# An elementwise multiply and GELU on one core: DRAM rows of 128 KB in two stores, with narrowing steps, in place of three contiguous pieces

## The chip, the cores and the metric

One core of one Trainium2 chip. The time is the device time of one execution in microseconds (us); quoted are medians. The kernels that are compared ran on the same chip, in turn.

## The reference

```python
x, y: (1024, 4096) float32
z = x * y
return 0.5 * z * (1 + tanh(sqrt(2 / pi) * (z + 0.044715 * z ** 3)))
```

33.55 MB are read and 16.78 MB written. The work is elementwise, so any assignment of elements to partitions is right if x, y and the output have the same.

## The kernel before

Each of the 128 partitions holds 32,768 columns of x in `xs`, where the product and the result overwrite it. y doesn't fit beside it and comes in three loads into a buffer of 20,440 columns; the second and third overwrite parts of the first that the multiplies have used. Columns of one *piece* lie in DRAM as one contiguous block, so a partition's row in the piece (1280, 17664) is 64 KB long and the next partition's follows it directly.

```python
PIECES = [(0, 1280), (1280, 17664), (17664, 32768)]
Y_LOADS = [(1280, 17664, 4056), (17664, 32768, 0), (0, 1280, 15104)]   # columns a:b, place in ys
Y_FREE = [0, 3, 4]                              # multiplies that must be done before the load
STEPS = [[4096] * 4, [2048] * 7 + [768], [1280]]
STORES = [(1280, 17664), (17664, 32768), (0, 1280)]

def columns(t, a, b):                           # piece [pa, pb) is contiguous in DRAM
    flat = t.flatten_outer_dims().rearrange("r c -> (r c)")
    pa, pb = next(q for q in PIECES if q[0] <= a and b <= q[1])
    return flat[P * pa : P * pb].rearrange("(p c) -> p c", p=P)[:, a - pa : b - pa]

_hoist(nc, [load_x(0).ins])                     # SyncE's queue, the very first
_hoist(nc, [load_x(1, nc.scalar).ins])          # ScalarE's queue
load_y(0)                                       # all others on SyncE's queue
load_x(2)
for i in range(1, len(Y_LOADS)):
    if Y_FREE[i]:
        nc.sync.wait_ge(sem_mul, Y_FREE[i])
    load_y(i)
# ... per step: VectorE xs = xs * ys, then ScalarE xs = gelu(xs) ...
for i, (a, b) in enumerate(STORES):
    if i == 0:
        nc.sync.wait_ge(sem_y[-2], 16)          # the first store waits for the second y load
    nc.sync.wait_ge(sem_act, done[b])
    nc.sync.dma_start(out=columns(out, a, b), in_=xs[:, a:b]).then_inc(sem_o[i], 16)
```

## Time and profile before

| | before |
|---|---|
| time, median (first 3 runs) | 119.83 us (119.72 to 119.94) |
| profiled execution, span | 118.3 us |
| VectorE, ScalarE busy | 35.2, 31.0 us |
| DMA queues, share of 16 engines | 82.2% + 16.5% |
| transfers, of which with 5 KB rows | 9, 3 |

A *packet* is one row of one partition, moved by one of the 16 DMA engines; a *wave* is 16 packets of one size, one per engine; a transfer has *landed* when its semaphore says that all of it is there.

Read the table from the bottom: the 16 DMA engines are full, so only two things can move the time, how many microseconds of rows each engine has to move, and any moment in which it moves none. The profile's lines stand in the prediction.

### The profile page before, as it was taken

What the parts mean: (1) busy time and instruction counts of PE and PEld (TensorE: products, weight loads), DVE (VectorE), ACT (ScalarE), POOL (GpSimd) and SP (SyncE); (2) the same over time, 40 slices, a digit from 0 to 9 for tenths busy, and PEclk for the clock granted to TensorE, in tenths of its full rate; (3) what the DMA queues carried; (4) which work ended last, traced back from release to release, by engine and by line L of the source; (5) the groups of instructions that cost most, each with busy time, mean ns of one, the idle gap of its engine ahead of it and who ended that gap; (6) DMA issues with size and microseconds to landing.
All of it is one profiled execution on the core that took longest, in us unless ns stands there. A gap on an engine that the chain in (4) does not pass through costs nothing.

```text
span 118.3 us, 82 instructions
## 1 busy us (share of the span) xinstructions
DVE 35.2 (30%) x13; ACT 31.0 (26%) x14; POOL 0.2 (0%) x4
## 2 busy tenths in 40 slices
DVE  0000000000000069999920000059999940000000
ACT  4000000000000001977974000007998990000000
POOL 0000000000000000000000000000000000000000
DMA  9888899889988897797797797798899889977975
GB/s 493 382 382 382 355 643 421 355 355 532 532 355 355 355 654 327 327 654 327 327 654 327 327 654 327 327 576 355 355 643 421 355 355 429 552 327 327 654 327 222
DMA packets 1296, 50.33 MB, mean 426 GB/s; under 512 B 144, under 2 KB 144, under 8 KB 528
## 3 DMA queue, kind: packets, MB, share of 16 engines
q1 hardware_dynamic: 1152, 41.94, 82.2%
q10 hardware_dynamic: 144, 8.39, 16.5%
HBM read 33.55 MB, written 16.78 MB: 426 GB/s over the span
## 4 chain that ended last, share of the span: by engine, by line
DMA 53%; DVE 24%; ACT 3%; issue 1%; DVEq 0%
DMA ys<-in_y_dram 53%; DVE xs L97 24%; ACT xs L105 3%; DVEq L94 0%
## 5 line engine op out<-in xcount | busy, mean ns | idle before, releaser
L97 DVE TENSOR_TENSOR xs<-xs,ys 128x2048 f32<-128x2048 f32 (+3 forms) x13 | 35.2, 2778 | 60.7 <-DMA ys<-in_y_dram 60.7
L105 ACT ACTIVATE xs<-xs 128x2048 f32<-128x2048 f32 (+3 forms) x13 | 29.7, 2301 | 64.9 <-DVE xs L97 64.9
L105 ACT ACT_TABLE_LOAD x1 | 1.3, 1283 | 1.6 <-PEq L59 1.6
L135 POOL MEMSET const-bfloat16-1.0<- 128x1 bf16 x1 | 0.1, 102 | 0.0
L135 POOL MEMSET const-uint8-127<- 128x1 uint8 x1 | 0.1, 102 | 0.0
L135 POOL MEMSET const-float32-0.0<- 128x1 f32 x1 | 0.1, 99 | 0.2 <-issue 0.2
L135 POOL MEMSET const-float32-1.0<- 128x1 f32 x1 | 0.1, 99 | 0.0
## 6 DMA issues: line engine op xcount, KB each, us to landing
xs<-in_x_dram SPq DMA_DIRECT2D x1, 7552.0 KB, 58.2
ys<-in_y_dram SPq DMA_DIRECT2D x1, 7552.0 KB, 22.5
out_dram<-xs SPq DMA_DIRECT2D x1, 7552.0 KB, 20.4
xs<-in_x_dram SPq DMA_DIRECT2D x1, 640.0 KB, 13.3
ys<-in_y_dram SPq DMA_DIRECT2D x1, 640.0 KB, 19.7
out_dram<-xs SPq DMA_DIRECT2D x1, 640.0 KB, 20.8
xs<-in_x_dram ACTq DMA_DIRECT2D x1, 32.5
ys<-in_y_dram SPq DMA_DIRECT2D x1, 40.7
```

The costliest lines, as they stand in the source:

```text
L97: nc.vector.tensor_mul(out=xs[:, c : c + w], in0=xs[:, c : c + w], in1=ys[:, r + c - a : r + c - a + w],).then_inc(sem_mul, 1)
L105: nc.scalar.activation(out=xs[:, c : c + w], in_=xs[:, c : c + w], func=GELU).then_inc(sem_act, 1)
L135: nc = _bacc.Bacc("TRN2", target_bir_lowering=False, num_devices=1)
```

## The change

Its intent: x, y and the output are seen as 128 rows of 128 KB, without the pieces. The output then leaves in two stores with equal rows of 64 KB, and no store of 5 KB rows is left at the end. Since all of the second half must be computed before its one store, the last steps are made narrow, so that ScalarE, which follows VectorE, has little left when VectorE ends. The small 5 KB loads remain: the heads of x first, the tails of y last.

```diff
-PIECES = [(0, 1280), (1280, 17664), (17664, 32768)]
-Y_LOADS = [(1280, 17664, 4056), (17664, 32768, 0), (0, 1280, 15104)]
+X_LOADS = [(0, 1280), (1280, 16384), (16384, 32768)]
+Y_LOADS = [(0, 16384, 4056), (16384, 31488, 0), (31488, 32768, 15104)]
-STEPS = [[4096] * 4, [2048] * 7 + [768], [1280]]
-STORES = [(1280, 17664), (17664, 32768), (0, 1280)]
+STEPS = [                                       # (y load, first column, width)
+    *((0, c, 4096) for c in range(0, 16384, 4096)),
+    (1, 16384, 1536), (1, 17920, 2048), (2, 31488, 1280),
+    *((1, c, 2048) for c in range(19968, 28160, 2048)),
+    (1, 28160, 1280), (1, 29440, 1024), (1, 30464, 640), (1, 31104, 384),
+]
+STORES = [(0, 16384), (16384, 32768)]
 def columns(t, a, b):
-    flat = t.flatten_outer_dims().rearrange("r c -> (r c)")
-    pa, pb = next(q for q in PIECES if q[0] <= a and b <= q[1])
-    return flat[P * pa : P * pb].rearrange("(p c) -> p c", p=P)[:, a - pa : b - pa]
+    return t.flatten_outer_dims().rearrange("(p a) c -> p (a c)", p=P)[:, a:b]
 # (cut: the loops over steps and stores, rewritten for the new tables, same waits)
```

More of the change, by code (lines that the diff above doesn't have):

```diff
@@ L10 @@
 GELU = mybir.ActivationFunctionType.Gelu_apprx_tanh
-PIECES = [(0, 1280), (1280, 17664), (17664, 32768)]
-Y_LOADS = [(1280, 17664, 4056), (17664, 32768, 0), (0, 1280, 15104)]
+COLUMNS = 32768
+X_LOADS = [(0, 1280), (1280, 16384), (16384, 32768)]
+Y_LOADS = [(0, 16384, 4056), (16384, 31488, 0), (31488, 32768, 15104)]
 Y_FREE = [0, 3, 4]
-STEPS = [[4096] * 4, [2048] * 7 + [768], [1280]]
-STORES = [(1280, 17664), (17664, 32768), (0, 1280)]
+STEPS = [
+    *((0, c, 4096) for c in range(0, 16384, 4096)),
+    (1, 16384, 1536),
+    (1, 17920, 2048),
+    (2, 31488, 1280),
+    *((1, c, 2048) for c in range(19968, 28160, 2048)),
+    (1, 28160, 1280),
+    (1, 29440, 1024),
+    (1, 30464, 640),
+    (1, 31104, 384),
+]
+STORES = [(0, 16384), (16384, 32768)]
 Y_BUF = 20440
@@ L51, in columns @@
     def columns(t, a, b):
-        flat = t.flatten_outer_dims().rearrange("r c -> (r c)")
-        pa, pb = next(q for q in PIECES if q[0] <= a and b <= q[1])
-        return flat[P * pa : P * pb].rearrange("(p c) -> p c", p=P)[:, a - pa : b - pa]
+        return t.flatten_outer_dims().rearrange("(p a) c -> p (a c)", p=P)[:, a:b]
     tc.close()
     tc.compile()
-    xs = nc.alloc_sbuf_tensor("xs", [P, PIECES[-1][1]], F32).ap()
+    xs = nc.alloc_sbuf_tensor("xs", [P, COLUMNS], F32).ap()
     ys = nc.alloc_sbuf_tensor("ys", [P, Y_BUF], F32).ap()
-    sem_x = [nc.alloc_semaphore(f"sem_x{i}") for i in range(len(PIECES))]
+    sem_x = [nc.alloc_semaphore(f"sem_x{i}") for i in range(len(X_LOADS))]
     sem_y = [nc.alloc_semaphore(f"sem_y{i}") for i in range(len(Y_LOADS))]
@@ L69, in load_x @@
     def load_x(i, engine=nc.sync):
-        a, b = PIECES[i]
+        a, b = X_LOADS[i]
         return engine.dma_start(out=xs[:, a:b], in_=columns(x, a, b)).then_inc(sem_x[i], 16)
@@ L86 @@
         load_y(i)
-    n = 0
-    done = {}
-    for i, (a, b, r) in enumerate(Y_LOADS):
-        for j, (xa, xb) in enumerate(PIECES):
-            if xa <= a < xb:
-                nc.vector.wait_ge(sem_x[j], 16)
-        nc.vector.wait_ge(sem_y[i], 16)
-        c = a
-        for w in STEPS[i]:
-            nc.vector.tensor_mul(
-                out=xs[:, c : c + w],
-                in0=xs[:, c : c + w],
-                in1=ys[:, r + c - a : r + c - a + w],
-            ).then_inc(sem_mul, 1)
-            n += 1
-            done[c + w] = n
-            nc.scalar.wait_ge(sem_mul, n)
-            nc.scalar.activation(
-                out=xs[:, c : c + w], in_=xs[:, c : c + w], func=GELU
-            ).then_inc(sem_act, 1)
-            c += w
+    waited = set()
+    for n, (i, c, w) in enumerate(STEPS, 1):
+        needed = [sem_y[i]] + [
+            sem_x[j] for j, (xa, xb) in enumerate(X_LOADS) if xa < c + w and c < xb
+        ]
+        for sem in needed:
+            if sem.num not in waited:
+                waited.add(sem.num)
+                nc.vector.wait_ge(sem, 16)
+        a, b, r = Y_LOADS[i]
+        nc.vector.tensor_mul(
+            out=xs[:, c : c + w],
+            in0=xs[:, c : c + w],
+            in1=ys[:, r + c - a : r + c - a + w],
+        ).then_inc(sem_mul, 1)
+        nc.scalar.wait_ge(sem_mul, n)
+        nc.scalar.activation(
+            out=xs[:, c : c + w], in_=xs[:, c : c + w], func=GELU
+        ).then_inc(sem_act, 1)
     for i, (a, b) in enumerate(STORES):
@@ L112 @@
             nc.sync.wait_ge(sem_y[-2], 16)
-        nc.sync.wait_ge(sem_act, done[b])
+        nc.sync.wait_ge(sem_act, max(n for n, (_, c, _) in enumerate(STEPS, 1) if a <= c < b))
         nc.sync.dma_start(out=columns(out, a, b), in_=xs[:, a:b]).then_inc(sem_o[i], 16)
```

## The prediction

> **What bounds the kernel now.** I read the first page for balance, then the DMA part for how many transfers there are, then stretches of the span for the rate, and last the chain of waits and the order in time around the first and last stores.
>
> ```profile
> span 118.3 us, 82 instructions
> DVE 35.2 (30%) x13; ACT 31.0 (26%) x14; POOL 0.2 (0%) x4
> DMA packets 1296, 50.33 MB, mean 426 GB/s; under 512 B 144, under 2 KB 144, under 8 KB 528
> ...
> q1 hardware_dynamic: 1152, 41.94, 82.2%
> q10 hardware_dynamic: 144, 8.39, 16.5%
> ```
>
> No compute engine is busy for a third of the span; the two DMA queues together take 98.7% of what 16 engines could give. 1296 packets are nine transfers of 128 rows and 16 semaphore writes. Three of them (the first x load, the last y load, the last store) have 5 KB rows: 3 x 128 = 384 of the 528 packets under 8 KB; the other 144 are the semaphore writes.
>
> The rate by stretch (the columns: stretch, its length, busy time of the three compute engines, the TensorE clock, the DMA share of 16 engines, GB/s; a packet is booked whole where it ends, which is why I chose stretches that hold exactly one wave of 16 packets):
>
> ```profile
> 1.00:118.00 117.00, 35.21 (x13) 31.01 (x14) 0.00 (x0) 1.00 1.00 430
> 80.50:82.50 2.00, 2.00 (x1) 1.83 (x1) 0.00 (x0) 1.00 1.21 524
> 99.50:102.00 2.50, 0.00 (x0) 0.00 (x0) 0.00 (x0) 1.00 0.89 387
> 116.40:117.60 1.20, 0.00 (x0) 0.00 (x0) 0.00 (x0) 1.00 1.02 418
> ```
>
> From 1 to 118 us the DMA engines are busy all the time. The second line is a wave of the first store: 524 x 2.00 = 1048 KB, which is 16 rows of 65,536 B, over 1.21 x 2.00 = 2.42 us on each engine. The third is a wave of the second store: 387 x 2.50 = 968 KB, 16 rows of 60,416 B, over 2.23 us. Both are 27.1 GB/s per engine, 433 GB/s for sixteen. The packet records of the trace say the same singly: 2,418 ns for 64 KB, 2,229 ns for 60,416 B, and 196 ns for most 5 KB rows. The first two differ by 5,120 B and 189 ns, so 5 KB cost 189 ns by size alone; as a row of its own it pays 7 ns more. Loads and stores have the same durations, and so have rows at a 64 KB pitch (x1, y0, the first store) and at 60,416 B. So at this rate DRAM isn't what limits; the 16 engines are.
>
> Then the end of the kernel, first the chain of waits (start, length, what), then the order in time:
>
> ```profile
> 55.54 22.47 DMA ys<-in_y_dram
> ...
> 78.10 1.52 DVE xs L97
> 79.62 0.68 issue
> 80.31 13.31 DVE xs L97 x6
> ...
> 93.64 3.80 ACT xs L105 x3
> ```
>
> ```profile
> 96.30 0.34 SPq L114 DMA_DIRECT2D out_dram<-xs  x1
> ...
> 97.46 0.33 SPq L114 DMA_DIRECT2D out_dram<-xs  x1
> ```
>
> The chain blames VectorE for 24% of the span, and that misleads. The second half of the compute (78.10 to 97.44) lies beside the first store, which is issued at 78.02. The packet records show that store's last rows ending between 98.27 and 98.51, and the second store's first rows starting on the same engines at 98.27 to 98.51, with no gap. The second store had been issued at 96.30, 2 us early; the third (5 KB rows) at 97.46, 18.7 us before its first packet at 116.13. The last packet ends at 117.88 and its semaphore comes at 118.25. Per engine the sum of rows is 3 x 8 x (2,418 + 2,229 + 196) = 116.23 us; from the first packet at 1.01 to the last at 117.88 are 116.87. The 0.64 left are mostly the offset between the engines' starts. There is practically no idle time to win.
>
> **What the Trainium skill says.** *DMA: Bandwidth & Descriptors*, "Where 436 GB/s comes from", puts the ceiling at 435 GB/s (16 ports); the trace's 433 agrees. The same page, "Latency and other measured facts", under "HBM row pitch at large powers of two", has copies with a per-partition pitch of 512 KiB at 207 GB/s per direction, 2 MiB at 164, full being 214. The changed kernel's pitch is 128 KB, a fourth of the mildest of these; the trace of before has no such pitch, only 64 KB, where nothing is lost. *ScalarE: Activation LUTs*, "What ACT_TABLE_LOAD costs", gives 186 ns + 0.833 ns per column for one ACTIVATE and an overlap of about 93 ns back to back. The trace agrees: 827 ns for 768 columns (826), 1,253 for 1280 (1,252), and the last three take 3.80 us where their durations sum to 3.99. *VectorE: DVE Perf Modes*, "Specifications", gives 0.96 GHz, 2,133 ns for 2048 columns at one a cycle; in the trace the starts are 2,202 ns apart, so one instruction costs columns/0.96 + 69 ns.
>
> **The change, part by part.**
>
> 1. *Bytes.* The same 50.33 MB. x is 5,120 + 60,416 + 65,536 B per row in place of 5,120 + 65,536 + 60,416; y has the same three sizes; the output is two stores of 64 KB rows for three. A row of 60,416 and one of 5,120 become part of one row of 65,536: 2,229 + 196 - 2,418 = 7 ns, eight rows per engine: **0.06 us less** on the path that sets the end. This is the only certain gain.
>
> 2. *Start of compute.* The first step needs x0, x1 and y0. Ahead of the compute there are now 8 x (196 + 2,229 + 2,418) = 38.7 us per engine and no longer 8 x (196 + 2 x 2,418) = 40.3, so the first multiply should start near 40.9 and not at 42.41. It saves nothing: the first store must stay behind the y loads in the queue, and until the end of the second y load the sum of rows is unchanged, so that one still lands near 78.0. The second and third y loads will be issued about 1.5 us earlier (near 54.0 and 58.4), both before the x load ahead of them ends at 59.8, so the queue doesn't run dry, as it doesn't now.
>
> 3. *First store.* Its issue after the landing at 78.0 is hidden by eight 5 KB rows (1.57 us per engine): issue at 78.02, first packets at 78.86 to 79.19. Unchanged.
>
> 4. *Second half of the compute.* Eleven steps for nine, 2 x 69 = 0.14 us more of VectorE. Starts from 78.10: the 1280 columns that follow the four of 2048 start at 92.18, then 93.58 (1024), 94.72 (640), 95.46 (384), end 96.01. ScalarE, with the formula above: 2048 until 94.21, then 1280 until 95.37, 1024 until 96.31, 640 until 96.93, 384 until **97.34**. So ScalarE, not VectorE, closes the half, and all of the second store waits for it: issue at 97.36. Now the corresponding store goes out at 96.30, so 1.06 us of the lead are lost. This is the one place where the change can cost time. From issue to first packet took 78.86 - 78.02 = 0.84 us, so the earliest packet can be at 98.20; the first engine becomes free at 98.27. It fits by 0.07 us. The narrowing widths are what makes it fit. I put the idle time at **0 to 0.2 us**.
>
> 5. *End.* Eight waves of 2,418 ns from 98.27 to 98.51 end at 117.61 to 117.85, in place of 117.88 at the latest; the semaphore about 0.37 us later, as now. One semaphore wait less on SyncE at the end, off the path.
>
> Sum: -0.06 + 0.0 to 0.2, on a median of 119.83: 119.8 to 120.0 by this account. Some of these waits may be half as large as I read them, so I take 119.8.
>
> **The rivals.**
>
> - *The 128 KB pitch slows DRAM.* For it: in both halves all rows now lie at one power of two, and the skill's page shows losses at pitches of powers of two. Against it: a 64 KB pitch loses nothing (2,418 ns, exactly what the size predicts), the engines run 0.2 to 0.5 us apart, which spreads their addresses, and the ceiling of the engines leaves DRAM some slack before a loss shows. 3% on every transfer would be 3.5 us, about 123.3; 3% on the stores alone 1.2 us, about 121.0. I give it one chance in fifteen of showing at all.
> - *The late second store leaves a hole.* If ScalarE ends later than I work out or the start of a transfer takes 1.2 us and not 0.84, all engines idle for some 0.4 us: 120.2. For it: the margin is 0.07 us. Against it: it needs an error in two durations that fit to some nanoseconds.
> - *Earlier compute or fewer small rows bring a real gain.* 1.5 us earlier compute would make 118.3, if it reached the end. Against it: the queue is full from 1.01 us on; VectorE gaining 1.5 us in the first half only waits longer for y1. A gain above 2% (under 117.4) needs a rate above 433 GB/s, which no stretch of whole waves shows.
>
> **Range and chances.** The before runs spread over 0.22 us; another chip or session may add as much. 119.4 to 120.4 takes in the gain of 0.06 with a fast session and the hole of 0.4 with a slow one; the pitch rival is outside it. Faster by over 2%: 1%. Slower by over 2% (over 122.2): only if all transfers lose by pitch, 3%.
>
> **What would show it.** Right: DMA packets 1152 (eight transfers), under 8 KB 384; a first multiply near 40.9; the second-half multiply still near 78.1; the second store issued near 97.4; waves of 64 KB still 2.42 us; DMA share near 1.0 up to 118. Wrong: 64 KB rows longer than 2.45 us (pitch), a share clearly below 1 around 98 us (hole), a y1 landing that isn't near 78.0 (then my reading of the queue is wrong).

## The result

| | before | after |
|---|---|---|
| median of 6 runs | 119.81 us (119.72 to 119.94) | 120.14 us (119.99 to 120.19) |
| profiled execution: time, span | 119.62, 118.3 us | 120.18, 118.8 us |
| second y load has landed | 78.00 | 78.63 |
| last store has landed | 118.25 | 118.81 |
| from the one to the other | 40.25 | 40.19 |

The ratio is 1.0026 (95% interval 1.0013 to 1.0039): the same within 2%, but slower by about 0.3 us. Ratios here are the mean time of one kernel's fast runs over that of the other's in the same rounds, so not quite the ratio of the medians quoted. The two profiled executions differ by 0.56 us, more than the medians; times inside a profile are compared with that in mind.

The page of the changed kernel, in the lines that answer those of before:

```profile
span 118.8 us, 83 instructions
DVE 35.3 (30%) x15; ACT 31.1 (26%) x16; POOL 0.2 (0%) x4
DMA packets 1152, 50.33 MB, mean 424 GB/s; under 512 B 128, under 2 KB 128, under 8 KB 384
...
q1 hardware_dynamic: 1008, 42.60, 83.4%
q10 hardware_dynamic: 144, 7.73, 15.0%
```

Eight transfers of 144 packets, the same bytes, the same compute. The stretches of the changed kernel (columns as in the prediction): the whole, one wave of the first store, one of the second.

```profile
1.00:118.00 117.00, 35.35 (x15) 31.09 (x16) 0.00 (x0) 1.00 1.00 430
81.00:83.00 2.00, 2.00 (x2) 1.28 (x2) 0.00 (x0) 1.00 1.21 524
...
100.00:102.40 2.40, 0.00 (x0) 0.00 (x0) 0.00 (x0) 1.00 1.01 437
```

A correction to the prediction first: it says that a packet is booked whole where it ends. It is booked where it *starts*; the wave in the second line starts at 81.94 by its packet records, that in the third at 101.31. A stretch that holds one whole wave reads the same either way, so the rates stand. Both waves are 16 rows of 64 KB in 2.42 us (1.21 x 2.00 and 1.01 x 2.40), as before. Rows at a 128 KB pitch are moved as fast as contiguous ones. So the rate in the body did not change.

The chain of waits of the changed kernel, and the issue of the second store from its order in time:

```profile
54.56 24.06 DMA ys<-in_y_dram
...
78.65 14.18 DVE xs L106 x7
...
92.86 5.05 ACT xs L112 x5
```

```profile
97.94 0.34 SPq L120 DMA_DIRECT2D out_dram<-xs  x1
```

54.56 + 24.06 = 78.62: the second y load lands 0.6 us later than before, and everything behind it moves with it: VectorE's half from 78.10 to 78.65, the second store's issue to 97.94. After that landing the changed kernel needs 0.06 us *less*. The time was lost before 78 us, in a stretch with the same bytes and the same waits (the sizes of the x and y loads only come in another order).

Most of it was lost in the first two microseconds. The kernel before, then the changed kernel, from 1 to 3 us:

```profile
1.00:2.00 1.00, 0.00 (x0) 0.43 (x1) 0.00 (x0) 1.00 0.95 374
2.00:3.00 1.00, 0.00 (x0) 0.85 (x1) 0.00 (x0) 1.00 2.68 1084
```

```profile
1.00:2.00 1.00, 0.00 (x0) 0.43 (x1) 0.00 (x0) 1.00 0.94 184
2.00:3.00 1.00, 0.00 (x0) 0.85 (x1) 0.00 (x0) 1.00 2.41 1006
```

In the first line of each only 5 KB rows of x start. The engines are as busy (0.95 and 0.94 of the time, the last column but one), yet the rows begun are 374 KB before and 184 KB after: 73 rows and 36. The same rows take longer. 190 KB less over 16 engines at 27.1 GB/s are 0.44 us per engine. (The 1084 and 1006 aren't rates: long rows of x that start there are booked whole; only stretches with short rows can be read as a rate.) The packet records show it singly. A 5 KB row takes 196 ns once the engines run; among the first ones of the changed kernel some took up to 1,001 ns, before at most 291. The last engine to begin its first long row of x did so at 3.31 us and not at 2.49. The packet records name no engine, so that one can't be followed. But the first long rows end 0.8 us apart over the 16 engines (before: 0.5), the last rows of the second y load still 0.7 us apart, the last of them at 78.18 and not at 77.64 (on average 0.4 us later than before), and the first store waits for that load as a whole.

### The profile page after: what moved, and what is told of

It reads as the page before. It is cut to its first block, busy times and chain, and to the rows that moved or that the text cites. A ratio compares the mean times of both kernels' runs of the same rounds, so it can differ in the third digit from the quotient of the medians.

```text
span 118.8 us, 83 instructions
## 1 busy us (share of the span) xinstructions
DVE 35.3 (30%) x15; ACT 31.1 (26%) x16; POOL 0.2 (0%) x4
## 4 chain that ended last, share of the span: by engine, by line
DMA 54%; DVE 23%; ACT 4%; issue 0%
DMA ys<-in_y_dram 54%; DVE xs L106 23%; ACT xs L112 4%
## 5 line engine op out<-in xcount | busy, mean ns | idle before, releaser
L106 DVE TENSOR_TENSOR xs<-xs,ys 128x2048 f32<-128x2048 f32 (+6 forms) x15 | 35.3, 2430 | 61.2 <-DMA ys<-in_y_dram 61.2
L112 ACT ACTIVATE xs<-xs 128x2048 f32<-128x2048 f32 (+6 forms) x15 | 29.8, 2018 | 65.3 <-DVE xs L106 65.3
```

What stands on the lines that cost most here:

```text
L106: nc.vector.tensor_mul(out=xs[:, c : c + w], in0=xs[:, c : c + w], in1=ys[:, r + c - a : r + c - a + w],).then_inc(sem_mul, 1)
L112: nc.scalar.activation(out=xs[:, c : c + w], in_=xs[:, c : c + w], func=GELU).then_inc(sem_act, 1)
```

## The experiments

**Theory A:** the 5 KB heads of x, which now lie 128 KB apart and not 5 KB, are read slowly at the start, and nothing makes that good. **Rival B:** the stores, the y tails or the late second store cost the time. Within A: is it the power of two, the spread, the first reading of a place, or only the first moment?

"Excess" below is the time of packets above their later duration (196, 2,229 or 2,418 ns), summed over all 16 engines; of each kernel's one profiled execution. Ratios are to the kernel before, in the same group of runs.

| run | excess of the first 16 packets | excess of those started by 6 us | second y load lands | from there to the end | median | ratio (95%) |
|---|---|---|---|---|---|---|
| before | 0.5 us | 4.1 | 78.00 | 40.25 | 119.81 | |
| changed | 4.9 | 9.1 | 78.63 | 40.19 | 120.14 | 1.0026 (1.0013 to 1.0039) |
| e1 heads together | 2.1 | 6.6 | 79.24 | 40.19 | 119.93 | 1.0015 (0.9992 to 1.0038) |
| e12 the same again | 2.4 | 5.1 | 78.40 | 40.17 | 119.95 | 1.0008 (0.9995 to 1.0021) |
| e2 before, heads apart | 7.6 | 10.1 | 78.72 | 40.23 | 120.16 | 1.0021 (1.0009 to 1.0033) |
| e3 rows of 64 KB | 7.6 | 12.3 | 78.86 | 40.22 | 120.43 | 1.0045 (1.0030 to 1.0059) |
| e4 heads 123 KB apart | 6.9 | 10.3 | 78.43 | 40.21 | 120.07 | 1.0013 (1.0001 to 1.0025) |
| e5 long rows first | 11.4 | 11.5 | 78.54 | 40.16 | 120.09 | 1.0015 (0.9995 to 1.0034) |
| e6 two x loads | 9.7 | 9.7 | 78.46 | 40.18 | 120.00 | 1.0012 (0.9990 to 1.0034) |
| e7 store not held | 9.7 | 13.3 | 78.98 | 40.65 | 120.91 | 1.0086 (1.0065 to 1.0107) |
| e8 wide steps | 7.1 | 9.1 | 78.53 | 41.14 | 121.05 | 1.0097 (1.0078 to 1.0116) |
| e11 even steps | 8.3 | 12.5 | 78.40 | 40.19 | 120.06 | 1.0026 (1.0012 to 1.0039) |

e1, e2, e3 and e4 shared one chip (the kernel before there: 119.89), e5 to e8 another (119.87), e9 to e12 a third (119.84).

### e1 and e12: the heads of x from one place

```diff
-return engine.dma_start(out=xs[:, a:b], in_=columns(x, a, b))...
+flat = x.flatten_outer_dims().rearrange("r c -> (r c)")
+src = columns(x, a, b) if i else flat[: P * 1280].rearrange("(p c) -> p c", p=P)
+return engine.dma_start(out=xs[:, a:b], in_=src)...      # wrong result on purpose
```

> The changed kernel, but the first x load takes its 128 rows of 5 KB from one contiguous 640 KB of x (wrong result on purpose). Theory A (heads lying 128 KB apart slow the first packets, up to 1001 ns where it was 291, one engine starts its first long row at 3.31 us and not at 2.49, and everything after is gated by that engine): first packets back to about 200 ns, second y load landing near 78.0, time 119.7 to 119.8, ratio to before 0.998 to 1.001. Rival B (the stores or y tails at the 128 KB pitch, or the later second store, cost the 0.3 us): time stays near 120.1, ratio 1.002 to 1.004.

Its profile fell on the slowest of its six executions (120.80; the others 119.71 to 120.17), in which rows were slow also between 6 us and the y landing: an excess of 16.4 us in sum, where the changed kernel has 1.1. So its 79.24 says nothing, and its interval holds both theories. I ran it again:

> The same kernel as the first run (heads of x from one contiguous 640 KB, wrong result on purpose), again, because its interval was too wide and its profile fell on its slowest execution. Theory A: below the changed kernel's 1.0026 and below the run of even steps beside it, ratio 0.998 to 1.0015. If the spread of the heads isn't the cause: equal to the run beside it, 1.002 to 1.004.

The second time the ratio is 1.0008 (0.9995 to 1.0021), beside 1.0026 for e11 in the same group; the medians are 0.04 (e1) and 0.11 us (e12) above the kernel before on their chips, e11's is 0.22 above beside e12, the changed kernel's 0.33 above in its own group. So the heads are half of the loss or more, as A says, but the intervals of e11 and e12 overlap, so by time alone it is likely and not settled. Two things that A expected did not come: the first packets don't go back to about 200 ns (the longest take 813 ns in e1 and 681 in e12), and e12's second y load lands at 78.40, just where e11's does, not near 78.0. Between 6 us and that landing the rows of e12 lose 4.0 us in sum, those of e11 0.45 and those of before 1.4; why is not shown. The clear test of A is the next run, which goes the other way. The stretch of e12 that answers the one above:

```profile
1.00:2.00 1.00, 0.00 (x0) 0.43 (x1) 0.00 (x0) 1.00 0.89 297
```

297, between 374 and 184. The time comes only part of the way back too.

### e2: the kernel before with its heads apart

```diff
+src = columns(x, a, b) if i else x.flatten_outer_dims().rearrange("(p a) c -> p (a c)", p=P)[:, 0:1280]
```

> The kernel before, but the first x load takes its 5 KB rows 128 KB apart (wrong result on purpose). Theory A: time 120.1 to 120.3, ratio 1.002 to 1.005, first packets up to about 1 us, second y load landing near 78.6. Rival B: nothing changes, ratio 0.999 to 1.001.

1.0021 (1.0009 to 1.0033), 120.16. This one edit puts the changed kernel's loss into the kernel before: longest of the first packets 1,058 ns, second y load at 78.72 (A gave 78.6). Its first stretch:

```profile
1.00:2.00 1.00, 0.00 (x0) 0.43 (x1) 0.00 (x0) 1.00 0.83 138
```

Three stores, old widths, contiguous long rows: B has none of its causes here, and the time is there all the same. A holds, B falls; the column "from there to the end" says it again, 40.23 to 40.25 for three stores and 40.16 to 40.22 for two, wherever the heads lie (e7 and e8, which change the stores' timing, aside).

### e3 and e4: is it the power of two?

```diff
 def columns(t, a, b):                                    # e3, right result
+    h = 0 if b <= 16384 else 16384                       # two contiguous halves
+    flat = t.flatten_outer_dims().rearrange("r c -> (r c)")
+    return flat[P * h : P * (h + 16384)].rearrange("(p c) -> p c", p=P)[:, a - h : b - h]
```

> The changed kernel with x, y and the output each as two contiguous halves, so rows are 64 KB apart and not 128 KB (right result). Theory A, if the cost is in the spread of the heads: the heads are now spread over 8 MB, so some of the 0.3 us remains: ratio 1.000 to 1.003. Rival C (the 128 KB pitch itself, in all transfers): ratio back to 0.999 to 1.001. By itself this run hardly decides; its first packets do: maximum under 300 ns for C, 300 to 1000 ns for A.

```diff
+src = columns(x, a, b) if i else flat[: P * 31488].rearrange("(p c) -> p c", p=P)[:, 0:1280]   # e4
```

> The changed kernel, but the first x load's 5 KB rows lie 123 KB (125,952 B) apart, no power of two (wrong result on purpose). If theory A works by the power of two (rows that start together meet at one place of DRAM): first packets near 200 ns, ratio 0.998 to 1.001. If by the mere spread over 16 MB (places in DRAM touched for the first time): as slow as the changed kernel, ratio 1.002 to 1.004.

Heads 123 KB apart, no power of two, lose as much at the start (10.3 us of excess, longest 1,101 ns) as heads 128 KB apart (9.1 and 10.1): the power of two isn't the cause. Rival C falls as well: at a 64 KB pitch the first packets are no better (12.3 us, longest 1,438), and after the second y load nothing differs. By time e4 isn't clear of e1 (their intervals overlap), and its ratio, 1.0013, lies below the 1.002 expected; the packets decide here. I had expected e3 between the other two, and it is the slowest of the four, 120.43. Its loss too lies before the y landing (78.86), but why heads over 8 MB should lose more than over 16 MB I can't say.

### e9 and e10: the first reading of a place, or the first moment?

```diff
 _hoist(nc, [load_x(0).ins])
+again = nc.sync.dma_start(out=ys[:, 0:1280], in_=columns(x, 0, 1280)).then_inc(sem_t, 16)   # e10: columns(y, ...)
+_hoist(nc, [again.ins])
-_hoist(nc, [load_x(1, nc.scalar).ins])
+load_x(1)
 load_y(0)
 # (cut: the second y load waits for sem_t)
```

> The changed kernel with all loads on SyncE's queue, and the 5 KB heads of x loaded twice in a row, the second time into a free part of the y buffer (right result, 0.66 MB more; read for its packets, not its time). Theory D (the cost belongs to reading a place for the first time): the first 128 packets exceed 196 ns by 6 to 13 us in sum, as in the changed kernel (8.7), the second 128, at the same addresses, by under 1.5 us. Rival E (rows so far apart are slow whenever short ones follow each other): both passes exceed by 6 us or more.

> As the run with the heads twice, but the second pass reads the 5 KB heads of y, which nothing has read before (result right: the extra copy is not used). Theory D: the second pass costs too, 3 to 13 us in sum over 196 ns each. Rival F (only the first microsecond of the DMA engines is slow, whatever they read): the second pass is under 1.5 us.

Both were run once, for their packets (122.27 and 122.12 us; they move 0.66 MB more on one queue). First e9, then e10; the first line has the beginning of the first pass, the second its rest, the third lies in the second pass:

```profile
1.00:2.00 1.00, 0.00 (x0) 0.08 (x1) 0.00 (x0) 1.00 0.96 118
2.00:3.00 1.00, 0.00 (x0) 1.00 (x1) 0.00 (x0) 1.00 0.99 389
3.40:4.40 1.00, 0.00 (x0) 0.00 (x0) 0.00 (x0) 1.00 1.01 420
```

```profile
1.00:2.00 1.00, 0.00 (x0) 0.08 (x1) 0.00 (x0) 1.00 0.91 143
2.00:3.00 1.00, 0.00 (x0) 1.00 (x1) 0.00 (x0) 1.00 1.03 420
3.40:4.40 1.00, 0.00 (x0) 0.00 (x0) 0.00 (x0) 1.00 1.03 430
```

No long row starts before 4.7 us here, so GB/s can be read directly: 118 and 143 in the first microsecond, then full rate. By packets the first pass has an excess of 11.8 us (e9) and 9.5 (e10), the second 0.03 and 0.05. E, "rows so far apart are always slow", falls. But D falls too: the heads of y had not been read before in this execution, lie just as far apart, and cost nothing in the second pass. And within the first pass 11.57 of the 11.79 us in e9, 9.09 of 9.51 in e10, lie in the first 32 packets, some two rows per engine; the rows after them are new places as well and take 196 ns. That looks like F, the first moment, with one thing that F doesn't say: in that moment it matters where the rows lie. Contiguous heads lose 0.5 to 2.4 us with the first 16 packets, heads far apart 4.9 to 10.4.

But the first moment isn't all of it either. In the kernel before, whose heads lie together, the first long rows of x, the first that lie far apart, are slow in place of the heads: all 16 take 2,458 to 2,780 ns where the size asks 2,418, 2.6 us in sum, though the engines have been at work for a microsecond by then. e1 and e12 lose 1.7 and 1.4 us on their first 16 long rows; the kernels with heads apart (the changed one, e2, e3, e4, e7, e8, e11) only 0.05 to 0.7. And in e9 and e10 some first long rows, at 5.3 us, take up to 2,761 and 2,785 ns for 2,229. So heads that lie together put part of the delay off to the long rows and make the sum smaller; they don't abolish it. What the delay is, and why most later rows don't have it, no run shows.

### e5 and e6: other loads first

```diff
-_hoist(nc, [load_x(0).ins])                    # e5
-_hoist(nc, [load_x(1, nc.scalar).ins])
+_hoist(nc, [load_x(1).ins])
+_hoist(nc, [load_x(0, nc.scalar).ins])
```

> The changed kernel, but the first two loads change queues: the 60,416 B rows of x go first on SyncE's queue, the 5 KB heads second on ScalarE's (right result). Theory A' (the cost is the first reading of spread places, paid once per row: eight heads in series per engine pay it up to five times before the long rows start): a long row pays it once, in 2.2 us of work, so the slowest engine is 0.6 to 1.0 us further on, second y load lands at 77.6 to 78.1, time 119.3 to 119.7, ratio 0.995 to 0.999. Rival (spread addresses cost the same total whatever comes first, or it is the start of the second queue): no change from the changed kernel, ratio 1.002 to 1.004.

```diff
-X_LOADS = [(0, 1280), (1280, 16384), (16384, 32768)]    # e6
+X_LOADS = [(0, 16384), (16384, 32768)]
-_hoist(nc, [load_x(1, nc.scalar).ins])
-load_y(0)
-load_x(2)
+_hoist(nc, [load_y(0, nc.scalar).ins])
+load_x(1)
```

> The changed kernel without the heads: x in two loads of 64 KB rows, the first on SyncE's queue, the first y load on ScalarE's (right result, seven transfers, 1008 packets). Theory A': as in the run with long rows first, and 0.06 us less for eight rows saved per engine: second y load lands at 77.5 to 78.0, ratio 0.994 to 0.999. Rival: 1.002 to 1.004.

My form A', that a long row would pay far less than five heads in series, failed. The first long row of each engine in e5 took 2,988 ns (median) where 2,229 is its size, 0.76 us more, and 3,067 for 2,418 in e6. The sums, 11.5 and 9.7 us, are those of the heads. Here each engine pays once, with whatever row comes first (the next 16 rows lose 0.01 us in sum); all rows that came first in these two runs lie far apart. e6 is 0.13 us above the kernel before, the changed kernel 0.33, but the intervals of e5 and e6 reach from below 1 to above the changed kernel's ratio. Neither is shown to beat the kernel before.

### e8 and e11: the margin of the second store

```diff
+    *((1, c, 4096) for c in range(16384, 28672, 4096)), (1, 28672, 2816), (2, 31488, 1280),          # e8
+    *((1, c, 2048) for c in range(16384, 30720, 2048)), (1, 30720, 768), (2, 31488, 1280),           # e11
```

> The changed kernel with the second half in steps of 4096, 4096, 4096, 2816, 1280 (right result). By the working of the prediction ScalarE ends at 98.97 (with this kernel's start at 78.65), the second store is issued at 98.99, its first packets come 0.84 us later at 99.83, where the engines are free from 98.90: a hole of 0.8 to 0.9 us, time 120.9 to 121.1, ratio 1.009 to 1.012. Rival (the engines make the hole good, or the issue is faster): 120.1 to 120.5.

> The changed kernel with the widths of the kernel before in the second half (seven of 2048, 768, 1280; right result). By the working for ScalarE the half ends 97.44 - 78.10 = 19.34 us after its start, where the changed kernel's takes 97.91 - 78.65 = 19.26: issue 0.08 us later, first packets at 98.86 where the engines are free at 98.90 (for a start at 78.65). Expected: no difference from the changed kernel, ratio to before 1.001 to 1.004. If narrowing is what hides the second store: a hole, 1.005 or more.

e8's second store in the order of time, then its stretches around the end of the first store (the first line has that store's last rows starting, the third the second store's first rows):

```profile
98.92 0.34 SPq L115 DMA_DIRECT2D out_dram<-xs  x1
```

```profile
96.30:96.60 0.30, 0.00 (x0) 0.30 (x1) 0.00 (x0) 1.00 8.07 3495
96.60:99.70 3.10, 0.00 (x0) 2.30 (x2) 0.00 (x0) 1.00 0.00 0
99.70:100.00 0.30, 0.00 (x0) 0.00 (x0) 0.00 (x0) 1.00 8.19 3495
```

A wave takes 2.42 us (8.07 x 0.30), but over 3.1 us pass in which none starts. By the packet records the engines become free at 98.80 to 98.98, and the next rows start at 99.76 to 99.92: 0.84 us after the issue, as worked out, and a hole of 0.94 to 0.98 us. "From there to the end" grows by 41.14 - 40.19 = 0.95, and the time is 121.05, within what was expected. A late second store costs its lateness, one for one.

e11 has the old widths. Its second store goes out at 97.79, 19.39 us after the second y load landed (78.40), the changed kernel's at 97.94, 19.31 after (78.63). Narrowing gains 0.08 us of lead, and it isn't needed: 120.06 and the ratio 1.0026 are the changed kernel's.

### e7: the first store not held back

```diff
-if i == 0:
-    nc.sync.wait_ge(sem_y[-2], 16)
```

> The changed kernel without the first store's wait for the second y load (the data it stores is complete at 63 us; it stays behind the y loads in the same queue; right result). If the wait merely passes on what the slowest engine lost: no gap at 79 us, slowest engine starts the store near 79.55 and not at 79.73, time 119.9 to 120.1. If the wait is what turns the loss at the start into time: 119.6 to 119.8. If it protects the order of transfers: slower.

The third case, slower: 120.91, ratio 1.0086. The store was issued at 62.57 and stood behind the y loads in the queue. The stretch around the end of the second y load, in which the third load's 5 KB rows should be starting, first e7, then the changed kernel:

```profile
77.75:78.50 0.75, 0.00 (x0) 0.00 (x0) 0.00 (x0) 1.00 0.63 130
78.50:79.50 1.00, 0.50 (x1) 0.00 (x0) 0.00 (x0) 1.00 0.93 312
```

```profile
77.75:78.50 0.75, 0.00 (x0) 0.00 (x0) 0.00 (x0) 1.00 1.00 416
78.50:79.50 1.00, 0.85 (x1) 0.00 (x0) 0.00 (x0) 1.00 1.15 478
```

130 GB/s of short rows are begun where it was 416 (the 478 has the first long rows of the store in it). With the store waiting in the queue, by the packet records, the last rows of the second y load took 2,536 ns (median, up to 3,020) and not 2,229, and a 5 KB row of the third up to 864. The store's own rows are then at 2,418 ns, but the engines keep their spread: the last rows end between 118.62 and 119.28, in the changed kernel between 118.25 and 118.40. So the wait, which looks like a loss, protects the loads in this kernel, and with it the engines are lined up again. That the slow rows are the same delay as at the start, met by the first rows written to a third region of DRAM, is possible; nothing here tests it.

## Why the prediction was right, and where it was not

The time, 120.14, lies in the range and in the class that had 96%; the point, 119.8, is 0.34 too low. That it lies in the range is in part luck: the upper part was left for a hole at 98 us in a slow session, and neither came; a loss at the start, which the sum didn't have, took that room. One of the prediction's own signs of being wrong, a second y landing that isn't near 78.0, did come.

1. *Bytes, 0.06 us less.* Held: 40.25 to 40.19 from the y landing to the end in the two profiles, 40.16 to 40.22 in the other kernels with two stores (e7 and e8 aside).
2. *Start of compute, second y load "near 78.0".* This is the step that failed: 78.63. Its sum of rows is right, and the queue did not run dry; it took for granted that the first rows take as long as all others. The term missing in the sum is the engines' start: 0.26 us per engine of excess before (4.1 / 16), 0.57 after (9.1 / 16), so 0.3 us more on average, and 0.8 us for the last engine's first long row (3.31 against 2.49). The first multiply came at 41.44 and not at 40.9 for the same reason. I had the first line of evidence in hand, the first packets of before with their 291 ns, and read it as nothing. The 0.64 us left over in its sum were read wrongly too, as mostly the offset between the engines' starts: the first 16 packets start within 0.23 us (1.01 to 1.24), while the excess of all packets of before is 0.48 us per engine.
3. *First store.* Held: issue at 78.64, first packets at 79.49, 0.85 us later.
4. *Second half.* ScalarE closed it at 92.86 + 5.05 = 97.91, 19.26 us after VectorE's start at 78.65; worked out had been 19.24 (97.34 - 78.10; the 2,133 ns in that working is an estimate from the clock, and the measured 2,202 carried it). No hole appeared: the second store's first rows start 3 ns after the first store's last. e8 shows that a later store would have cost its lateness, e11 that the widths weren't needed for it.
5. *The pitch rival.* I let a loss by pitch fall on all transfers or all stores. It fell on none of the waves in the body (2.42 us). A loss from far-apart rows did come, at the start alone; but e4 shows that it isn't one of powers of two, so the rival was wrong in its mechanism as well.

The sum in hindsight: -0.06 for the rows, +0.3 to +0.4 for the start. The cause of the loss, heads of x that lie far apart, is shown by e2; e1 and e12 make it likely and no more. What stays open: why the start depends on where the rows lie, why e3 loses more than the changed kernel, and why e12 gets back only part of the time.

## What to carry to other kernels

When the DMA engines are full from end to end, look at the first two microseconds and at the hand-overs: in these runs the first rows, above all where they lay far apart, showed delays that most later rows didn't, and the engines carried their lateness to the next wait for a whole transfer. A first load from one compact block of DRAM (about 0.3 us by e2), and the store kept back until the loads have landed (about 0.7 us by e7), were worth more here than one transfer fewer (0.06 us). A store that must wait for all of a half cost nothing here as long as it was issued 0.85 us before the engines ran out; beyond that, in e8, it cost its lateness.

## What the Trainium skill lacked or had wrong

- *DMA: Bandwidth & Descriptors*, "Latency and other measured facts", has a first-byte latency of about 600 ns for this path. The runs show 0.84 to 0.85 us from the start of the issuing instruction (which takes 0.34) to the first packet (the first stores of before and changed, the second of e8), and 1.01 at the start of the kernel; the page doesn't say from where it counts. It has nothing on a delay of the first rows that depends on where they lie: 0.6 to 0.7 us more per engine in e5 and e6, once, where the partitions' rows lie 128 KB apart, and almost nothing (0.5 us over 16 engines) in the first 16 packets of one contiguous block in the kernel before.
- The same section's "HBM row pitch at large powers of two": no run here goes to 512 KiB. At 128 KB pitch 64 KB rows keep their 2,418 ns.
- No page has that a store which waits in the queue behind loads slows the loads' last rows (2,536 ns for 2,229, and about 0.7 us of time, in e7).
